# Normalised rows and projection weights as scaled float16 pairs, rows of all four token groups kept on chip

## The chip, the cores and the metric

The kernel runs on one core of a Trainium2 chip. The metric is the device time of one execution in microseconds. The core's engines have short names in the profile: PE is TensorE's matrix products (PEld its weight loads), DVE is VectorE, ACT is ScalarE, POOL is GpSimd, and SP issues the DMAs.

## The reference

Two layers over 2048 tokens of 1024 features. Each layer projects the normalised rows by one matrix, splits the result into a gated spatial part (u, v, g_A) and an attention part (q, k, v, g_B), and adds the normalised output projection to its input.

```python
for l in range(DEPTH):                       # DEPTH = 2, x is (1, 2048, 1024)
    h = rmsnorm(x, pre_g[l])                 # x / rms(x) * pre_g
    proj = jnp.einsum('bsd,de->bse', h, w_in[l])
    u_a, v_a, g_a, q, k, v, g_b = jnp.split(proj, idx, axis=-1)   # 512,512,512,512,128,128,512
    y_a = gmlp_group(u_a, v_a, ...) * jax.nn.silu(g_a)
    y_b = gqa_axial_attention(q, k, v, ...) * jax.nn.silu(g_b)    # 8 query heads, 2 kv heads
    out = jnp.einsum('bse,ed->bsd', jnp.concatenate([y_a, y_b], -1), w_out[l])
    x = x + rmsnorm(out, post_g[l])
```

Inside the attention q and k are RMS-normalised by head, multiplied by a gain and rotated (rope); `gmlp_group` applies a layer norm to v and mixes the 128 positions of a chunk by a 128x128 matrix per head. All of it is float32.

## The kernel before

A float32 operand of a product is kept as a pair, hi and lo, and a product is three passes, hi·hi, hi·lo and lo·hi (`PASSES`). In the projections both are of the type fp32r, four bytes each: ACT casts the high part and DVE subtracts it from the original for the low part.

The 2048 tokens are four groups of 512, each of four tiles of 128. `hT_jobs` prepares a group: a tile's rows (`x_t`, or `x_h` where the layer before has prepared them) are loaded, their squares summed by ACT, a reciprocal root found in tiny DVE instructions (`rs_x`, L133 to L137), and the rows multiplied by it and by `g_row`, the gain pre_g on every partition (L308). PE transposes them, ACT casts the result to `hT`, and DVE forms the low part (L319).

The projection weights come in blocks of 256 columns: K/V, two of Q, two of VA (v_a), two of GB (g_B), and four pairs of 128 columns of g_A and of u. `load_w` loads a block (`w_raw`), `split_w` splits it into `w_hi` (ACT, L276) and `w_lo` (DVE, L277), two instructions of 128x1024 each. `proj_tok` makes 24 products of 128x256 per tile and block, `proj_ch` 24 of 128x512 per group and 128 columns for the gates.

One layer goes through the tokens in two halves of two groups. A half's stages are: K/V and first Q block for each of its groups, second Q block, both VA blocks, both GB blocks, then the gate blocks; each half loads and splits every block anew. I call K/V and the two Q blocks the front. The next half's first group is prepared among the last gate blocks. Every stage ends in work on the other engines: `norm_rope` for K and Q has ACT square, DVE sum (L360), nine tiny DVE instructions, then the rope: a DVE product with PSUM (L367), a GpSimd product (L369), eight DVE products per tile pair on quarter rows (L372) and a DVE addition (L374), after which PE transposes the result. The tables of the rope are loaded and multiplied with a gain on GpSimd (L351).

A background list, `bg`, sets where much of that stands in the program: a job is added with a delay in ticks, and one tick passes after every eight products of `proj_tok` or four of `proj_ch`. Q's transposes have a delay of 16 (`Q_DELAY`), K's of 20 and more. Eight PSUM banks hold everything that PE produces, seven of them taken in turn. During the second half's GB and gate stages 128 products `pmax` and their maxima `mx` (L706) for the attention are mixed in. The attention and the output projection follow; at the end of layer 0 the last tiles are finished by GpSimd products with `g_post`, and rows of groups 0 and 1 are already normalised for layer 1 (`x_r`).

The functions that the change touches:

Of the kernel before, what the change touches and what calls it, by code (L numbers as in the profile page):

```python
# [19 lines left out]
P = 128  # L20
D = 1024
# [13 lines left out]
NORM_SCALE = -8192.0 / D ** 0.5  # L35


@with_exitstack
def encoder(ctx: ExitStack, tc, x, w_in, w_out, pre_g, post_g, ln_a_g, ln_a_b,
# [7 lines left out]
    HALF = min(2, NG)  # L47
# [49 lines left out]
    nc.vector.tensor_scalar_mul(two, two, 2.0)  # L97
    one_h = const.tile([P, 32], F16, name="one_h")
# [76 lines left out]
    class Project:  # L175
        def __init__(self, l):
            self.l = l
            self.stores = []
            self.g_row = None

        def norm_row(self):

            self.g_row = lay.tile([P, D], F32, name="g_row")
            if self.l == 0:
                for i in range(2):
                    sl = slice(i * GRP, (i + 1) * GRP)
                    one = f_t("g_one")[0:1]
                    nc.sync.dma_start(one, pre_g[self.l:self.l + 1, sl])
                    ps = ps_t("pt")
                    PE.matmul(ps, ones1, one, start=True, stop=True)  # L190
                    nc.vector.tensor_scalar(self.g_row[:, sl], ps, 1.0 / NORM_SCALE, None, ALU.mult)
                return
            nc.sync.dma_start(self.g_row, pre_g[self.l].partition_broadcast(P))
            nc.gpsimd.tensor_scalar(self.g_row, self.g_row, 1.0 / NORM_SCALE, None, ALU.mult)

        def begin(self):

            self.w_kv = self.split_w(self.load_w([C_K]), 2)

        def gains(self):  # L200
            l = self.l
            self.two = lay.tile([P, 32], F32, name="two_v")
            self.gain_q = lay.tile([P, 2, HD], F32, name="gain_q")
# [66 lines left out]
        def split_w(self, raw, n=4):  # L270

            hi = w_t([P, ND, WB], "w_hi")
            lo = w_t([P, ND, WB], "w_lo")
            for d in range(0, ND, n):
                sl = slice(d, d + n)
                nc.scalar.copy(hi[:, sl], raw[:, sl])  # L276
                nc.vector.tensor_tensor(lo[:, sl], raw[:, sl], hi.bitcast(F32)[:, sl], ALU.subtract)  # L277
            return hi, lo

        def hT_jobs(self, g, tail=False):  # L280

            hT = [big_t([P, 2, ND // 2, GRP], "hT") for _ in range(2)]
# [3 lines left out]
            def prep(j):  # L286
                def f():
# [10 lines left out]
                    if self.g_row is None:  # L298
                        self.norm_row()
# [7 lines left out]
                    for i in range(2):  # L307
                        nc.vector.scalar_tensor_tensor(xt[i], xt[i], z, self.g_row[:, i * GRP:(i + 1) * GRP],  # L308
                                                       ALU.mult, ALU.mult)
                return f  # L310

            def trans(j, q):
                def f():
                    ps = ps_t("pt").rearrange("p (d t) -> p d t", d=4)
                    for d in range(4):
                        PE.transpose(ps[:, d, :], xs[j][q][:, d * P:(d + 1) * P], ident)
                    sl = slice(j * P, (j + 1) * P)
                    act.copy(hT[q][:, 0, :, sl], ps)
                    dve.tensor_tensor(hT[q][:, 1, :, sl], ps, hT[q].bitcast(F32)[:, 0, :, sl], ALU.subtract)  # L319
                return f  # L320
            return hT, [prep(j) for j in range(TPG)], [trans(j, q) for j in range(TPG) for q in range(2)]

        def proj_tok(self, hT, j, w, ps=None, c0=0):
# [3 lines left out]
            for a, b in PASSES:  # L327
                for d in range(ND):
                    PE.matmul(ps[:, c0:c0 + WB], hT[d // 4][:, a, d % 4, j * P:(j + 1) * P], w[b][:, d, :],
                              start=(n == 0), stop=(n == 3 * ND - 1))  # L330
                    n += 1
                bg.tick()
            return ps

        def proj_ch(self, hT, w, c0):
            ps = ps_t("pp")
            n = 0
            for a, b in PASSES:
                for d in range(ND):
                    PE.matmul(ps, w[b][:, d, c0:c0 + P], hT[d // 4][:, a, d % 4, :],  # L340
# [13 lines left out]
        def norm_rope(self, banks, n, tb):  # L354
# [7 lines left out]
            nc.vector.tensor_scalar(msf, msf, 1.0 / HD, EPS, ALU.mult, ALU.add)  # L362
# [23 lines left out]
        def do_kv(self, g, banks):  # L386
            k_st, k_lo, v32, _ = self.kv
            b4 = [ps.rearrange("p (t h d) -> p t h d", t=2, d=HD) for ps in banks]
            for i, ps in enumerate(b4):
                t = g * TPG + 2 * i  # L390
                nc.scalar.copy(v32[:, t:t + 2], ps[:, :, 2:4])
            krs = self.norm_rope([ps[:, :, 0:2] for ps in b4], NKV, self.rope_rows(g, self.gain_k))
# [15 lines left out]
        def do_q(self, g, banks, b):  # L408
            qrs = self.norm_rope([ps.rearrange("p (t h d) -> p t h d", t=2, d=HD) for ps in banks], 4,
                                 self.rope_rows(g, self.gain_q))  # L410
# [55 lines left out]
        def do_gate(self, g, c, pg, pu):  # L466
# [3 lines left out]
            nc.scalar.activation(th, pg, AF.Tanh, scale=0.5)  # L470
            nc.vector.scalar_tensor_tensor(th, th, 1.0, pg, ALU.add, ALU.mult)
            nc.vector.tensor_tensor(th, pu, th, ALU.mult)
            nc.vector.scalar_tensor_tensor(th, th, 0.5, z, ALU.mult, ALU.mult)
# [7 lines left out]
        def do_gb(self, g, banks, b):  # L481
            for i, ps in enumerate(banks):
                th = f_t("fa")
                nc.scalar.activation(th, ps, AF.Tanh, scale=0.5)
# [4 lines left out]
        def scale_v(self):  # L489
# [18 lines left out]
            def scale():  # L508
# [5 lines left out]
                nc.vector.tensor_scalar(self.two, two, e, None, ALU.mult)  # L514

# [14 lines left out]
        def run(self, kv, first, last_jobs, first_wo):  # L530
# [3 lines left out]
            halves = [list(range(h, min(h + HALF, NG))) for h in range(0, NG, HALF)]  # L534
            w_kv = self.w_kv
            for n, gs in enumerate(halves):
                if len(gs) > 1:
                    hTs[gs[1]], preps, trans = self.hT_jobs(gs[1])
                    late = self.l == 0 and n == 0
                    for j, f in enumerate(preps):  # L540
                        if late:
                            bg.add(8 + j, f)
                        else:
                            f()
                    for m, f in enumerate(trans):
                        bg.add((13 if late else T_DELAY) + 3 * m // 2, f)
                if n == 0:
                    self.gains()
                raw = self.load_w([C_Q])
                if self.l == 0 and n == 0:  # L550
                    w = []
                    bg.add(8, lambda w=w, raw=raw: w.extend(self.split_w(raw)))
                else:
                    w = self.split_w(raw)
                for i, g in enumerate(gs):
                    if i == 0:
                        for f in self.stores:
                            f()
                        self.stores = []
                    if i == len(gs) - 1:  # L560
                        raw = self.load_w([C_Q + WB])
                    self.do_kv(g, self.banked(hTs[g], w_kv))
                    if i == len(gs) - 1:
                        w_next = self.split_w(raw)
                        raw = self.load_w([C_VA])
                    self.do_q(g, self.banked(hTs[g], w), 0)
                if n == 0:
                    self.spatial_weights()
                w = w_next
                for i, g in enumerate(gs):  # L570
                    self.do_q(g, self.banked(hTs[g], w), 1)
                    if i == 0:
                        w_next = self.split_w(raw)
                w = w_next
                raw = self.load_w([C_VA + WB])
                ws = [row_t("ws", dt=F32R) for _ in range(2)]
                for i in range(2):
                    nc.sync.dma_start(ws[i].bitcast(F32), ws_d[:, i])
                w = [w, self.split_w(raw)]
                raw = self.load_w([C_GB])  # L580
                for g in gs:
                    vs = []
                    for j in range(TPG):
                        ps = self.proj_tok(hTs[g], j, w[0])
                        self.proj_tok(hTs[g], j, w[1], ps, WB)
                        v = f_t("fv")
                        nc.scalar.copy(v, ps)
                        vs.append(v)
                    self.do_va(g, vs, ws)
                w = self.split_w(raw)  # L590
                blocks = [[C_GB + WB]] + [[C_GA + c * P, C_U + c * P] for c in range(4)]
                if n + 1 < len(halves):
                    blocks.append([C_K])
                if n + 1 == len(halves):
                    nc.gpsimd.memset(self.kv[1][HD:HD + 2], 1.0)
                    self.scale_v()
                    last_jobs()
                for b in range(2):
                    raw = self.load_w(blocks.pop(0))
                    for i, g in enumerate(gs):  # L600
                        self.do_gb(g, self.banked(hTs[g], w), b)
                        if i == 0:
                            w_next = self.split_w(raw)
                    w = w_next
                more = n + 1 < len(halves)
                order = [(c, i) for c in range(4) for i in range(len(gs))]
                if more:
                    order[-2 * len(gs):] = [(c, i) for i in range(len(gs)) for c in (2, 3)]
# [645 lines left out]
```

## Time and profile before

| | |
|---|---|
| median of 3 runs | 2741.04 us (2739.78 to 2742.96) |
| span of the profiled execution | 2737.6 us (the runs are 2 to 5 us above it) |
| PE busy | 2666.4 us, 97% |
| DVE busy | 1858.2 us, 68% |
| ACT busy | 1523.9 us, 56% |
| POOL busy | 1296.1 us, 47% |
| read from HBM, written | 176.57 MB, 85.07 MB |
| w_raw loads | 28 of 1024 KB, 32 of 512 KB |

Layer 0's projections lie between 17.6 and 616.2 us, layer 1's between 1383.5 and 1966.4 us, and what is left is attention and output projection. A busy time is the union of an engine's instructions; matrix products overlap, so that their mean duration (287 ns for 128x256) is longer than the distance at which one follows the other, and the distance is read from the starts in the timeline.

### The profile page before, as it was taken

The page shows a single profiled execution, that of the slowest core. Times are in us where ns is not written, and L with a number is a line of the kernel's source. Part 1 is how long each engine was busy: PE and PEld are TensorE (multiplying, and loading weights), DVE is VectorE, ACT ScalarE, POOL GpSimd, SP SyncE. Part 2 cuts the span into 40 slices and gives each one's busy share as a digit, 9 for nine tenths or more (in the row PEclk, how much of TensorE's full clock was granted, in tenths as well). Part 3 has the DMA queues.
Part 4 walks back from the last instruction along what each step waited for, and adds up shares of the span by engine and source line. Part 5 has one row for each costly group of instructions (what it writes and reads, how often), then busy time and mean ns, then how long its engine had stood idle before and what let it go on. Part 6 is the DMA issues. An engine that isn't in the chain of part 4 may idle for free.

```text
span 2737.6 us, 48445 instructions
## 1 busy us (share of the span) xinstructions
PE 2666.4 (97%) x18234; PEld 1773.2 (65%) x18234; DVE 1858.2 (68%) x3780; ACT 1523.9 (56%) x3023; POOL 1296.1 (47%) x1079
## 2 busy tenths in 40 slices
PE   7999999999999999999999999999999999999997
PEld 7998999764444444445599989997644444444444
DVE  7762888876666766666497538897766656666664
ACT  5221422118887777877642224221388878778774
POOL 1210121008786776777633011210377767767764
PEclk9999999999999999999999999999999999999998
DMA  4434422322232222222354434232312222221313
GB/s 137 149 98 122 161 80 84 107 75 84 81 91 66 76 84 84 90 81 84 125 169 138 122 115 144 74 121 71 109 51 81 79 71 70 83 75 48 114 46 132
DMA packets 275170, 264.78 MB, mean 97 GB/s; under 512 B 19188, under 2 KB 233332, under 8 KB 274936
## 3 DMA queue, kind: packets, MB, share of 16 engines
q1 hardware_dynamic: 274936, 261.70, 30.5%
q8 instruction: 143, 2.34, 0.4%
q14 instruction: 91, 0.75, 0.1%
HBM read 176.57 MB, written 85.07 MB: 96 GB/s over the span
## 4 chain that ended last, share of the span: by engine, by line
PE 81%; DVE 10%; ACT 5%; DMA 2%; issue 2%; POOL 1%; SPq 0%; DVEq 0%; POOLq 0%; ACTq 0%
PE pp L84 28%; PE sp L84 14%; PE pout L84 12%; PE po L84 12%; PE pmax L84 7%; PE sums L84 4%; PE pt L84 3%; ACT p_parts L84 2%; ACT p_f L84 2%; DVE fc L372 1%; DVE w_lo L277 1%; DVE mx L84 1%; DVE p_parts L84 1%; DVE o_t L84 1%; DVE mx L706 1%
## 5 line engine op out<-in xcount | busy, mean ns | idle before, releaser
L84 POOL TENSOR_TENSOR p_parts<-p_f,p_parts 128x512 f16<-128x512 f32 x872 | 1037.4, 1208 | 395.1 <-ACT p_f L84 295.5
L84 ACT ACTIVATE p_parts<-sp 128x512 f16<-128x512 f32 x1024 | 628.3, 614 | 295.7 <-PE sp L84 288.5
L84 DVE TENSOR_REDUCE mx<-pmax 128x1 f32<-128x512 f32 x768 | 511.2, 681 | 230.9 <-PE pmax L84 228.9
L84 PE MATMUL pout<-wo,y_t 128*128 128x512 f32 x1488 | 655.4, 504 | 1.0 <-ACT p_f L84 0.7
L84 PE MATMUL po<-p_parts,v_st 128*32 128x512 f16 (+1 forms) x3072 | 637.2, 382 | 0.2
L84 ACT ACTIVATE p_f<-sp 128x512 f32<-128x512 f32 x1024 | 629.9, 615 | 0.4 <-DVE p_parts L84 0.4
L84 PE MATMUL pp<-w_hi,hT 128*128 128x256 f32 x3584 | 496.7, 287 | 2.1 <-DVE k_t L405 1.1
L84 PEld LDWEIGHTS pp<-w_hi,hT 128*128 128x128 f32 x3584 | 457.3, 192 | 6.4 <-issue 1.3
L84 PE MATMUL pmax<-k_t,q_m 128*128 128x512 f16 x1024 | 388.9, 381 | 12.5 <-DVE mx L84 7.4
L84 PE MATMUL sp<-q_st,k_t 128*128 128x512 f16 x1024 | 389.2, 380 | 5.3 <-ACT p_f L84 2.9
L84 PEld LDWEIGHTS <-v_st 128*32 128x32 f16 (+1 forms) x3072 | 193.1, 96 | 308.4 <-issue 250.3
L84 PE MATMUL sp<-q,k_t 66*128 66x512 f16 x1024 | 390.1, 381 | 0.0
L84 PEld LDWEIGHTS pout<-wo,y_t 128*128 128x128 f32 x1488 | 280.7, 190 | 134.2 <-issue 14.9
L84 PEld LDWEIGHTS <-k_t 128*128 128x128 f16 (+1 forms) x2048 | 191.3, 98 | 184.1 <-issue 71.1
L477 POOL TENSOR_TENSOR fl<-fa,fh 128x512 fp32r<-128x512 f32 x32 | 42.7, 1335 | 539.6 <-ACT fh L476 496.0
L84 PE MATMUL pp<-hT,w_hi 128*128 128x512 f32 x1024 | 273.1, 413 | 0.0
L84 PE MATMUL pp<-w_lo,hT 128*128 128x256 f32 x1792 | 260.0, 288 | 0.0
L84 PE MATMUL sums<-p_parts,one_h 128*32 128x512 f16 x2048 | 241.8, 379 | 0.0
L84 PEld LDWEIGHTS pp<-w_lo,hT 128*128 128x128 f32 x1792 | 232.9, 192 | 1.0
L84 PEld LDWEIGHTS pp<-hT,w_hi 128*128 128x128 f32 x1024 | 192.8, 189 | 35.1
L706 DVE TENSOR_REDUCE mx<-pmax 128x1 f32<-128x512 f32 x256 | 172.5, 687 | 49.1 <-PE pmax L84 47.5
L84 PEld LDWEIGHTS <-q_m 128*128 128x128 f16 x1024 | 99.8, 98 | 142.6 <-issue 41.8
(165 smaller groups left out, 2778.1 us busy)
## 6 DMA issues: line engine op xcount, KB each, us to landing
w_raw<-in_w_in_dram SPq DMA_DIRECT2D x28, 1024.0 KB
y_t<-y_d SPq DMA_DIRECT2D x56, 512.0 KB
w_raw<-in_w_in_dram SPq DMA_DIRECT2D x32, 512.0 KB
x_t<-in_x_dram SPq DMA_DIRECT2D x16, 512.0 KB
z_d<-fb SPq DMA_DIRECT2D x32, 256.0 KB
gb_d<-fa SPq DMA_DIRECT2D x32, 256.0 KB
fb<-z_d SPq DMA_DIRECT2D x32, 256.0 KB
y_d<-fh SPq DMA_DIRECT2D x32, 256.0 KB
```

Source lines behind the costliest of these rows:

```text
L84: return tc.keep_in_program_order(call(*args, **kw))
L277: nc.vector.tensor_tensor(lo[:, sl], raw[:, sl], hi.bitcast(F32)[:, sl], ALU.subtract)
L372: nc.vector.tensor_tensor(t2[:, :, :, lo:lo + 16], qn[:, :, :, hi:hi + 16], tbi[:, :, 1:2, lo:lo + 16].broadcast_to([P, 2, n, 16]), ALU.mult)
L477: nc.gpsimd.tensor_tensor(lo, th, hi.bitcast(F32), ALU.subtract)
L706: dve.tensor_reduce(s.mx[:, j, c:c + 1], ps, AX.X, ALU.max)
```

## The change

1. Rows and weights of the projections are float16 pairs. `hT` is one tile [hi/lo, 8, 512] in place of two, so that four groups fit where two did. `w_hl` holds both parts of a block in half of the bytes.
2. `pre_g` no longer multiplies the rows (`g_row`) but the weights, as a column per partition (`g_col`, L277 after), on GpSimd but for one half of layer 0's first Q block.
3. Since float16 has a narrow range, each block is scaled by a power of two from its largest magnitude: two DVE reductions (L280), a DVE square, two tiny PE products with a constant (`pe`), and eight tiny DVE instructions (L289 to L303). ACT casts with that scale, DVE forms the low part with it (L295). What stands behind the projections takes the scale back (`w.u`, `w.hu`, `w.hu2`, `w.eps`, `two_g`).
4. Each block is loaded and split once per layer: a layer is now K/V and first Q block for all four groups, second Q block for all, VA for all, GB, gates. Group 2's rows are prepared in the front like the others. The part of `split_w` after the reductions is delayed by 14 ticks (`W_DELAY`).

```diff
-        def split_w(self, raw, n=4):
-            hi = w_t([P, ND, WB], "w_hi")
-            lo = w_t([P, ND, WB], "w_lo")
-            for d in range(0, ND, n):
-                sl = slice(d, d + n)
-                nc.scalar.copy(hi[:, sl], raw[:, sl])
-                nc.vector.tensor_tensor(lo[:, sl], raw[:, sl], hi.bitcast(F32)[:, sl], ALU.subtract)
-            return hi, lo
+        def split_w(self, raw, delay, vec=False):
+            w = Obj()
+            w.hl = w_t([P, 2, ND, WB], "w_hl", F16)
...
+            for i in range(2):
+                sl = slice(i * ND // 2, (i + 1) * ND // 2)
+                engine = nc.vector if vec and i == 0 else nc.gpsimd
+                g = self.g_col[:, sl].unsqueeze(2).broadcast_to([P, ND // 2, WB])
+                engine.tensor_tensor(raw[:, sl], raw[:, sl], g, ALU.mult)
+            for i in range(2):
+                sl = slice(i * ND // 2, (i + 1) * ND // 2)
+                nc.vector.tensor_reduce(top[:, i:i + 1], raw[:, sl].rearrange("p d e -> p (d e)"), AX.X, ALU.max,
+                                        apply_absolute_value=True)
+            nc.vector.tensor_tensor(sq, top, top, ALU.mult)
+
+            def rest():
+                ps = ps_t("pe")
+                for i in range(2):
+                    PE.matmul(ps[:, 0:1], spread_w, sq[:, i:i + 1], start=(i == 0), stop=(i == 1))
...
+                for i in range(2):
+                    sl = slice(i * ND // 2, (i + 1) * ND // 2)
+                    nc.scalar.activation(w.hl[:, 0, sl], raw[:, sl], AF.Copy, scale=w.e)
+                    nc.vector.scalar_tensor_tensor(w.hl[:, 1, sl].rearrange("p d e -> p (d e)"),
+                                                   raw[:, sl].rearrange("p d e -> p (d e)"), w.e,
+                                                   w.hl[:, 0, sl].rearrange("p d e -> p (d e)"),
+                                                   ALU.mult, ALU.subtract)
...
+            if delay is None:
+                rest()
+            else:
+                bg.add(delay, rest)
+            return w
 
         def hT_jobs(self, g, tail=False):
 
-            hT = [big_t([P, 2, ND // 2, GRP], "hT") for _ in range(2)]
+            hT = big_t([P, 2, ND, GRP], "hT", F16)
...
-                        nc.vector.scalar_tensor_tensor(xt[i], xt[i], z, self.g_row[:, i * GRP:(i + 1) * GRP],
-                                                       ALU.mult, ALU.mult)
+                        nc.vector.tensor_scalar(xt[i], xt[i], z, None, ALU.mult)
...
+            for i, g in enumerate(gs):
...
+                if i + 1 < NG:
+                    start(g + 1)
+                if i == 1:
+                    raw = self.load_w([C_Q + WB])
+                self.do_kv(g, self.banked(hTs[g], w_kv), w_kv)
+                if i == 2:
+                    w_next = self.split_w(raw, W_DELAY)
+                    raw = self.load_w([C_VA])
+                self.do_q(g, self.banked(hTs[g], w[0]), 0, w[0])
...
+            for i, g in enumerate(gs):
+                if i == 0:
+                    va = [self.split_w(raw, W_DELAY)]
+                    raw = self.load_w([C_VA + WB])
+                if i == 2:
+                    va.append(self.split_w(raw, W_DELAY))
+                    raw = self.load_w([C_GB])
+                self.do_q(g, self.banked(hTs[g], w), 1, w)
...
-                    return lambda: DVE.scalar_tensor_tensor(s.x[:, sl], s.o[:, sl], zh, nxt.g_row[:, sl],
-                                                            ALU.mult, ALU.mult)
+                    return lambda: DVE.tensor_scalar(s.x[:, sl], s.o[:, sl], zh, None, ALU.mult)
```

A scheduler sets the order on each engine, and it moves three places that matter here. On DVE at the start of the program, before: the low parts of K's weights stand among the steps of the first row's root.

```order
L191 TENSOR_SCALAR g_row<-pt 128x512
L277 TENSOR_TENSOR w_lo<-w_raw,w_hi 128x512
L133 TENSOR_SCALAR rs_m<-ss_x 128x1
L134 TENSOR_SCALAR rs_x<-rs_m 128x1
L136 TENSOR_SCALAR rs_t<-rs_x,rs_m 128x1
L277 TENSOR_TENSOR w_lo<-w_raw,w_hi 128x512
```

The same place after:

```order
L280 TENSOR_REDUCE w_col<-w_raw 128x1 x2
L282 TENSOR_TENSOR w_col<-w_col 128x2
L289 TENSOR_SCALAR w_col<-pe 128x1
L290 TENSOR_SCALAR w_col<-w_col 128x1
```

After those and the remaining tiny steps the two L295 follow, and the first row's root stands behind all of them; the reductions wait for GpSimd's product of the weights.

On GpSimd, in the front of layer 0, before: the rope table of K (`fa`), the filling of a constant, and the first rope products.

```order
L351 TENSOR_TENSOR fa<-fa,gain_k 128x512
L595 MEMSET k_t 2x4096
L369 TENSOR_TENSOR fc<-fc,fa 128x2x128 x2
L351 TENSOR_TENSOR fa<-fa,gain_q 128x512
L369 TENSOR_TENSOR fc<-fc,fa 128x512 x2
```

After (L382 is before's L351, L400 is L369, L643 is L595):

```order
L277 TENSOR_TENSOR w_raw<-w_raw,g_col 128x1024 x3
L382 TENSOR_TENSOR fa<-fa,gain_k 128x512
L277 TENSOR_TENSOR w_raw<-w_raw,g_col 128x1024 x2
L643 MEMSET k_t 2x4096
L277 TENSOR_TENSOR w_raw<-w_raw,g_col 128x1024 x2
L400 TENSOR_TENSOR fc<-fc,fa 128x2x128 x2
L382 TENSOR_TENSOR fa<-fa,gain_q 128x512
L400 TENSOR_TENSOR fc<-fc,fa 128x512 x2
```

K's weights and one half of Q0's come first, then Q1's and VA0's ahead of the first rope product.

On GpSimd, where layer 1 begins, before:

```order
L84 TENSOR_TENSOR o_t<-o_t,g_post 128x256 x16
L351 TENSOR_TENSOR fa<-fa,gain_k 128x512
L595 MEMSET k_t 2x4096
L369 TENSOR_TENSOR fc<-fc,fa 128x2x128 x2
L351 TENSOR_TENSOR fa<-fa,gain_q 128x512
```

And after:

```order
L84 TENSOR_TENSOR o_t<-o_t,g_post 128x256 x16
L277 TENSOR_TENSOR w_raw<-w_raw,g_col 128x1024 x2
L382 TENSOR_TENSOR fa<-fa,gain_k 128x512
L643 MEMSET k_t 2x4096
L277 TENSOR_TENSOR w_raw<-w_raw,g_col 128x1024 x3
L400 TENSOR_TENSOR fc<-fc,fa 128x2x128
```

Q0's products stand behind the 16 gains of layer 0's last tiles, and three of the four for Q1 and VA0 ahead of the first rope product.

More of the change, by code (lines that the diff above doesn't have):

```diff
@@ L178, in __init__, with norm_col @@
             self.stores = []
[L179 to L194, printed above, removed]
+            self.g_col = None
+        def norm_col(self):
+            self.g_col = lay.tile([P, ND], F32, name="g_col")
+            nc.sync.dma_start(self.g_col, pre_g[self.l].rearrange("(d p) -> p d", p=P))
         def begin(self):
-            self.w_kv = self.split_w(self.load_w([C_K]), 2)
+            raw = self.load_w([C_K])
+            if self.g_col is None:
+                self.norm_col()
+            self.w_kv = self.split_w(raw, None)
         def gains(self):
@@ new lines, in run, with start, one @@
+            gs = list(range(NG))
+            left = {}
+            def start(g):
+                hTs[g], preps, trans = self.hT_jobs(g)
+                left[g] = list(trans)
+                def one():
+                    if left[g]:
+                        left[g].pop(0)()
+                late = self.l == 0 and g == 1
+                for j, f in enumerate(preps):
+                    if late:
+                        bg.add(8 + j, f)
+                    else:
+                        f()
+                for m in range(len(trans)):
+                    bg.add((13 if late else T_DELAY) + 3 * m // 2, one)
@@ new lines, in run @@
+            nc.gpsimd.memset(self.kv[1][HD:HD + 2], 1.0)
+            self.scale_v()
+            last_jobs()
+            blocks = [[C_GA + c * P, C_U + c * P] for c in range(4)]
+            gbs = []
+            for b in range(2):
+                assert w.ready
+                gbs.append(w)
+                for i, g in enumerate(gs):
+                    self.do_gb(g, self.banked(hTs[g], w), b, w)
+                    if i == 1:
+                        w_next = self.split_w(raw, W_DELAY)
+                        raw = self.load_w(blocks.pop(0))
+                w = w_next
@@ new lines, in run @@
+            assert self.scaled
+            for b in range(2):
+                nc.vector.tensor_scalar(self.two_g[:, b], self.two, gbs[b].e, NORM_SCALE, ALU.mult, ALU.mult)
+            for c in range(4):
+                assert w.ready
+                for i, g in enumerate(gs):
+                    pg = self.proj_ch(hTs[g], w, 0)
+                    pu = self.proj_ch(hTs[g], w, P)
+                    self.do_gate(g, c, pg, pu, w)
+                    if i == 1 and c < 3:
+                        w_next = self.split_w(raw, W_DELAY)
+                        raw = self.load_w(blocks.pop(0)) if blocks else None
+                    if c == 3:
+                        hTs[g] = None
+                        if i == 1:
+                            first_wo()
+                w = w_next
@@ L635, in encoder @@
+            bg.flush()
     KK_DELAY = 20
@@ L749, in den @@
                 for c in range(4):
-                    PE.matmul(s.pd[32 * c:32 * c + 32, 0:TPG], layers[l].two, rows[:, :, c, 0], start=True, stop=True)
+                    PE.matmul(s.pd[32 * c:32 * c + 32, 0:TPG], layers[l].two_g[:, h // 4], rows[:, :, c, 0], start=True, stop=True)
             def rden():
```

194 lines of the change are left out of this document (77 added, 117 removed).

## Prediction

> **What bounds the kernel now.** I read the page first: the engine shares, the slices, the chain.
>
> ```profile
> PE 2666.4 (97%) x18234; PEld 1773.2 (65%) x18234; DVE 1858.2 (68%) x3780; ACT 1523.9 (56%) x3023; POOL 1296.1 (47%) x1079
> ...
> PE   7999999999999999999999999999999999999997
> ...
> DVE  7762888876666766666497538897766656666664
> ...
> PE 81%; DVE 10%; ACT 5%; DMA 2%; issue 2%; POOL 1%; SPq 0%; DVEq 0%; POOLq 0%; ACTq 0%
> ```
>
> TensorE is busy 97% and carries 81% of the chain, DMA 2%: halving the weight loads buys nothing by itself. But VectorE is high in slices 1 to 8 and 20 to 24, where the projections run. So the windows of the projection stages next: the start, then the four fronts (K/V and both Q blocks of a half), then the four value stages, then the GB and gate stages. Columns: stretch, its length, busy time of PE, PEld, DVE, ACT, POOL.
>
> ```profile
> 0.00:17.60 17.60, 5.47 (x12) 2.73 (x12) 8.88 (x33) 7.34 (x16) 0.69 (x6) 1.00 0.63 205
> ...
> 17.60:107.70 90.10, 83.47 (x674) 81.80 (x673) 80.11 (x225) 36.66 (x80) 23.52 (x16) 0.98 0.36 110
> 310.50:389.90 79.40, 76.34 (x641) 75.96 (x640) 70.92 (x183) 27.28 (x57) 22.06 (x16) 1.00 0.36 114
> 1383.50:1460.40 76.90, 76.90 (x650) 76.90 (x649) 70.00 (x183) 26.10 (x54) 25.80 (x22) 1.00 0.37 119
> 1663.10:1740.00 76.90, 76.15 (x641) 75.95 (x640) 69.28 (x176) 27.22 (x57) 19.26 (x15) 1.00 0.35 111
> sum 323.30, PE 312.86 PEld 310.62 DVE 290.31 ACT 117.26 POOL 90.63; mean PE 78.22 PEld 77.66 DVE 72.58 ACT 29.32 POOL 22.66
> ...
> sum 220.90, PE 220.11 PEld 214.45 DVE 157.24 ACT 59.98 POOL 47.17; mean PE 55.03 PEld 53.61 DVE 39.31 ACT 15.00 POOL 11.79
> ...
> 165.10:310.50 145.40, 144.12 (x860) 128.25 (x859) 70.91 (x158) 40.83 (x76) 15.32 (x11) 1.00 0.45 134
> 442.90:616.20 173.30, 172.52 (x967) 134.48 (x967) 142.65 (x258) 33.18 (x56) 15.37 (x11) 1.00 0.33 97
> ...
> sum 637.30, PE 633.16 PEld 525.37 DVE 427.04 ACT 147.92 POOL 62.21; mean PE 158.29 PEld 131.34 DVE 106.76 ACT 36.98 POOL 15.55
> ```
>
> Value, GB and gate stages are plain TensorE (853.3 of 858.2 us). The fronts have two near-bounds: TensorE 312.9 of 323.3 and VectorE 290.3. VectorE is even behind at their ends. The last rope addition (L374) starts 18.4 us after the last front's end at 1740.0, and the windows of these lags show what it then does:
>
> ```profile
> L374 DVE TENSOR_TENSOR fc<-fc x12: 408/674/680, 1683.2 to 1758.4; 128x512 f32<-128x512 f32 x8, 128x256 f32<-128x256 f32 x4
> ...
> 389.90:408.90 19.00, 18.74 (x158) 18.54 (x156) 17.82 (x41) 5.06 (x9) 5.98 (x4) 1.00 0.32 94
> ...
> sum 76.20, PE 75.62 PEld 69.91 DVE 65.64 ACT 27.77 POOL 26.08; mean PE 18.91 PEld 17.48 DVE 16.41 ACT 6.94 POOL 6.52
> ```
>
> Four times 65.64/4 = 16 us of front work is done under the value stage. I take 0.2% (5.5 us) as what a measurement here can tell from no change.
>
> **What TensorE gains.** Eight 256-column fp32r products start 0.96 us before the next eight, 120 ns each; sixteen of 512 columns 3.62 us, 226 ns each. Float16 is seen at 512 only: from 704.31 to 706.27 nine products, 218 ns each.
>
> ```profile
> 150.37 1.12 PE L84 MATMUL pp<-w_hi,hT 128*128 128x256 f32 x8
> 151.33 1.12 PE L84 MATMUL pp<-w_lo,hT 128*128 128x256 f32 x8
> ...
> 250.44 3.79 PE L84 MATMUL pp<-hT,w_hi 128*128 128x512 f32 x16
> 254.06 1.98 PE L84 MATMUL pp<-hT,w_lo 128*128 128x512 f32 x8
> ...
> 704.31 0.39 PE L84 MATMUL sp<-q_st,k_t 128*128 128x512 f16 x1
> ...
> 706.27 0.38 PE L84 MATMUL sp<-q,k_t 66*128 66x512 f16 x1
> ```
>
> So 8 ns less per product at 512. At 256 no row tells: 0 if nothing changes, 8 if the gain is a fixed part of each product, 11 if the product takes half of 218; I take 10. Outside the fronts a layer has 768 value and 768 GB products at 256 and 768 gate products at 512: 15.4 + 6.1 = 21.5 us, 43 for both layers. Group 2's 32 transposes leave the gate stage (the first GB/gate window holds them), at no more than the 120 ns of 256 columns some 3.5 us a layer: 7. The second GB/gate window is 27.9 us longer than the first for its 128 pmax products, which are float16 and worth 128 × 218 ns = 27.9, although the first has those 3.5 us of transposes more: so about 3.5 us a layer goes where the two types alternate, 0 to 7 in all, take 3. The attention's x_r loses its gain row: 16 times 1134 less 543 ns (rows below) on VectorE, mostly covered there by TensorE, 0 to 9, take 2. Sum **55 us** (22 to 70).
>
> **What the fronts lose.** Rows first, VectorE's and GpSimd's: groups of instructions (busy us, mean ns of one, idle before), three lines by tile (shortest/median/longest in ns, first and last start in us) and one of the timeline.
>
> ```profile
> L706 DVE TENSOR_REDUCE mx<-pmax 128x1 f32<-128x512 f32 x256 | 172.5, 687 | 49.1 <-PE pmax L84 47.5
> ...
> L277 DVE TENSOR_TENSOR w_lo<-w_raw,w_hi 128x1024 fp32r<-128x1024 f32 x84 | 104.1, 1253 | 17.2 <-ACT w_hi L276 16.0 <-PE pp L84 0.6
> L372 DVE TENSOR_TENSOR fc<-fc,fa 128x128 f32<-128x128 f32 x128 | 68.0, 590 | 16.3 <-POOL fa L351 15.7
> L308 DVE SCALAR_TENSOR_TENSOR x_t<-x_t,rs_x,g_row 128x512 f32<-128x512 f32 x48 | 37.6, 822 | 0.1
> L137 DVE TENSOR_SCALAR rs_x<-rs_t,rs_x 128x1 f32<-128x1 f32 x72 | 14.1, 210 | 0.7
> ...
> L84 DVE SCALAR_TENSOR_TENSOR x_r<-o_t,rs_o,g_row 128x512 f32<-128x512 f32 x16 | 18.1, 1134 | 0.0
> ...
> L277 DVE TENSOR_TENSOR w_lo<-w_raw,w_hi x92: 680/1218/1923, 10.9 to 1891.8; 128x1024 fp32r<-128x1024 f32 x84, 128x512 fp32r<-128x512 f32 x8
> ...
> L438 DVE TENSOR_SCALAR fv<-fv,mv_v,rs_y x32: 539/543/1529, 141.4 to 1800.6; 128x512 f32<-128x512 f32 x32
> L372 DVE TENSOR_TENSOR fc<-fc,fa x192: 209/279/1392, 54.9 to 1757.6; 128x128 f32<-128x128 f32 x128, 128x64 f32<-128x64 f32 x64
> ...
> L369 POOL TENSOR_TENSOR fc<-fc,fa 128x512 f32<-128x512 f32 x32 | 48.7, 1523 | 63.0 <-DVE fc L367 56.3 <-issue 6.1
> L477 POOL TENSOR_TENSOR fl<-fa,fh 128x512 fp32r<-128x512 f32 x32 | 42.7, 1335 | 539.6 <-ACT fh L476 496.0 <-issue 43.6
> ...
> 1375.33 11.94 POOL L84 TENSOR_TENSOR o_t<-o_t,g_post 128x256 f32<-128x256 f32 x15 [0.49 <-ACT pout L84]
> ```
>
> VectorE's work for all fronts before is 8.9 (start) + 290.3 + 65.6 (lags). The preparation of group 2, in the gate stage before, comes to stand in the front: the first GB/gate window has 70.9 of DVE, the second 142.7 with 128 maxima of 0.687 (88), so 54.7 without, and the first also holds one K split of 2 × 1.25: 13.7 us, 27.4 for both layers. Together 392.
>
> Out go 17 splits (five and four in layer 0, four and four in layer 1) of two w_lo of 1.253: −42.6. In come 9 of the new kind: two reductions of 1024 elements (0.7 to 1.4; take 1.2), two L295 of 1.25 as w_lo, nine tiny ones of 0.15 to 0.21 (1.5): 6.4 each, +57.6; and one weight product on VectorE, 1.3. The row scale x_t drops a vector operand: 822 to the 543 of fv, which also has one vector and per-partition scalars; 48 × 0.279 = −13.4.
>
> The gain products move to GpSimd: 17 in the fronts of 2 × 1335 = 2.7 us (2.4 to 3.3), 46 us. GpSimd has room, but VectorE pays: L372 takes 209 ns at best and 590 on average, 128 × 0.38 = 48.8 us lost beside 48.7 us of GpSimd's L369. There the two always meet; a weight product meets such two-operand work some 3 times in 10 (L372, L374 and the like are some 120 of 392 us): +14, bounds 0 and 46.
>
> The Trainium skill, page "SBUF — State Buffer", section "Who interferes with whom", says that a VectorE instruction with two SBUF inputs and a GpSimd instruction that reads SBUF take a port from one another for the whole instruction, and that one with a single SBUF input or a reduction does not; the L372 row agrees. By it the price reaches the upper bound if the scheduler puts each product ahead of two-operand work, a sum 34 us higher (rival 3); the order doesn't tell which meet.
>
> Sum of VectorE's work: 392 − 42.6 + 57.6 + 1.3 − 13.4 + 14 = **409 us**. TensorE's in the fronts is 312.9 − 2304 × 10 ns (768 + 384 a layer, all at 256) + 7 = 297. So VectorE becomes the bound there. When it is behind it is busy 17.82 of 19.0, 0.94: 409/0.94 = 435. It begins about 12.5: K's first w_lo started at 10.9, after a cast, and a product of 2.7 now stands in that place. The lag that the value stage can take is unchanged in kind (Q's transposes follow 16 ticks later and wait for L374), but there is one value stage per layer in place of two: 2 × 16 = 32 come off. At the start of layer 1 Q0's products stand behind the 16 gains on GpSimd, the last of which ends at 1387.3, and the K rope's L400 behind those and Q1's; TensorE has K/V of one group (96 × 110 ns) meanwhile; the Q0 block then waits for products, reductions and split: some 5 us (0 to 12). Fronts after: 12.5 + 435 − 32 + 5 = 420.5; before 17.6 + 323.3 = 340.9. Loss **80 us** (40 to 125).
>
> Other edits: the loads in layer 0 of Q1 and VA0 stand behind four row loads that wait for buffers, and K's first rope product waits on GpSimd behind both; L372, which follows it in the rope, first ran at 54.9 before, and two loads of 1 MB at the front's 110 GB/s take 19 us, so they land before that if issued by 35: nothing. Two tiny products per block on TensorE wait for the reductions 14 ticks later: nothing, since 14 ticks are 12 us. ACT's casts keep their number per split.
>
> **Sum.** −55 + 80 = +25 on the span of 2737.6: 2762.6. The median of the three runs, 2741.04, stands 3.4 above this span, so 2766.
>
> **Rivals.** (1) VectorE keeps up better, faster: fewer gaps (0.99) and no meeting on the port, 395/0.99 = 399, fronts 379, +38.5 − 55: 2724. For it: fronts before had it at 0.90 because TensorE gave the pace; against: 0.94 even when behind. It decides below 410 us of work over efficiency, where the fronts take 396 and both sums cancel, 25 us under mine. (2) TensorE stays the bound in the fronts: 297 + 22 for the start = 319, −22 − 55: 2664. VectorE's work would need to be a quarter smaller; the windows speak against. (3) Port fully paid, +32/0.94 = 34: 2800. (4) Float16 doesn't shorten 256-column products, so that part of the change doesn't do what it says: value and GB gain 31 us less: 2797. For it: no row at 256. (5) Both sums cancel: 2741.
>
> **Chances.** My forecast 0.46, own range 2747 to 2795; (1) 0.26; (2) 0.06; (3) 0.07; (4) 0.03; (5) 0.12. Faster (1, 2) 0.32, same (5) 0.12, slower 0.56. The range 2690 to 2805 leaves out (2), the tail of (1), and what lies beyond (3).
>
> **What would show it.** Right: in the K/V and Q stage of each layer DVE busy over 90% and PE clearly under (some 0.75), PE's waits there on DVE L405 and L350; that stage some 185 to 215 us a layer; value stages with no f32 pp, 256-column pitch near 110 ns; gate blocks of 48 products near 10.4 us instead of 10.9; L277 on POOL 2.4 to 3.3; mean of L403 above 590. Wrong: PE above 0.95 in the fronts (rivals 1, 2), a pitch of 120 (4), or a stall of TensorE on `pe` products, or of GpSimd on a weight load, over 10 us, which I have at nothing.

## The result and the profile after

The changed kernel takes 2789.06 us (median of 4 runs, 2788.33 to 2790.26) where the kernel before took 2740.41 beside it. The ratio is 1.0174, with a 95% interval of 1.0159 to 1.0188: slower by 49 us. The forecast was 2766, 25 us slower.

The page of the changed kernel: shares of the engines, and the slices of PE, DVE and the granted clock.

```profile
PE 2626.5 (94%) x18318; PEld 1543.7 (55%) x18318; DVE 1891.0 (68%) x3978; ACT 1500.0 (54%) x3007; POOL 1361.8 (49%) x1121
...
PE   5788999999999999999978889999999999999997
...
DVE  7978797435665766666498878983366656566664
...
PEclk9899999999999999999999999999999999999999
```

PE is busy 40 us less in a span that is 49 us longer. It is at 5 to 8 tenths in the first four slices and at 7 and 8 in the 21st to 24th, where the two layers begin. The clock's digit drops to 8 in the second slice only, but the windows below show 0.90 and 0.92 for both fronts (0.98 to 1.00 before). The windows of the changed kernel by stage: the start, the two fronts (K/V and Q blocks of four groups), then per layer the value stage, and GB with the gates. Columns as in the prediction: stretch, length, busy time of PE, PEld, DVE, ACT, POOL, granted clock.

```profile
0.00:26.20 26.20, 2.76 (x12) 2.50 (x12) 13.15 (x46) 7.34 (x14) 7.77 (x10) 1.00 0.62 196
26.20:235.10 208.90, 172.69 (x1393) 146.65 (x1393) 185.81 (x530) 77.99 (x180) 58.37 (x40) 0.90 0.31 95
1404.20:1611.20 207.00, 166.14 (x1370) 141.62 (x1369) 184.18 (x485) 69.93 (x156) 67.09 (x50) 0.92 0.32 99
...
235.10:347.60 112.50, 106.09 (x925) 93.74 (x923) 85.90 (x220) 24.31 (x51) 31.74 (x22) 0.97 0.22 62
347.60:637.30 289.70, 288.14 (x1755) 172.37 (x1754) 181.93 (x346) 53.28 (x83) 35.73 (x25) 1.00 0.29 84
...
sum 806.40, PE 788.98 PEld 532.56 DVE 535.19 ACT 155.07 POOL 135.08; mean PE 197.25 PEld 133.14 DVE 133.80 ACT 38.77 POOL 33.77
```

| stage, both layers | before | after | difference | forecast |
|---|---|---|---|---|
| start and fronts | 340.9 | 442.1 | +101.2 | +79.6 |
| value, GB, gates | 858.2 | 806.4 | −51.8 | −53 |
| span | 2737.6 | 2786.9 | +49.3 | +25 |

What is left between these sums (attention and output projection) is unchanged within 1 us. The loss in the fronts is a quarter larger than forecast. In the fronts DVE is busy 370.0 of 415.9 us and PE 338.8.

The gain behind the fronts came as forecast in its sum, but not in its parts. The two value stages together became 5.6 us longer (226.5 beside 220.9), where the terms of the forecast make them some 15 us shorter, and GB and gates became 57.4 us shorter (579.9 beside 637.3) in place of some 38. About 7 us of both comes from where the boundary lies: 29 of the 120 ns products a layer now stand before it. But in the two value stages TensorE also waits 13.7 us for VectorE's last rope additions (L405), and before it was busy 220.1 of 220.9 us there.

The float16 products can now be read in the timeline (start, length, count):

```profile
269.83 5.84 PE L84 MATMUL pp<-w_hl,hT 128*128 128x256 f16 x52
275.43 0.48 PE L84 MATMUL pt<-ws,fh 128*128 128x256 f32 x2
...
511.70 33.40 PE L84 MATMUL pp<-hT,w_hl 128*128 128x512 f16 x154
```

52 products of 256 columns take 5.60 us to the next instruction, 108 ns each (120 before); 154 of 512 columns 33.40 us less the last one's 0.38, 216 ns each (226 before).

### The profile page after: what moved, and what is told of

It reads as the page before. It is cut to its first block, busy times and chain, and to the rows that moved or that the text cites. A ratio compares the mean times of both kernels' runs of the same rounds, so it can differ in the third digit from the quotient of the medians.

```text
span 2786.9 us, 48753 instructions
## 1 busy us (share of the span) xinstructions
PE 2626.5 (94%) x18318; PEld 1543.7 (55%) x18318; DVE 1891.0 (68%) x3978; ACT 1500.0 (54%) x3007; POOL 1361.8 (49%) x1121
## 5 line engine op out<-in xcount | busy, mean ns | idle before, releaser
L84 PE MATMUL pp<-w_hl,hT 128*128 128x256 f16 x5376 | 675.5, 279 | 9.9 <-DVE hT L350 5.8
L84 PEld LDWEIGHTS <-hT 128*128 128x128 f16 x5376 | 527.7, 100 | 105.7 <-issue 14.0
L84 PE MATMUL pp<-hT,w_hl 128*128 128x512 f16 x1536 | 344.4, 379 | 0.0
L84 PEld LDWEIGHTS <-w_hl 128*128 128x128 f16 x1536 | 150.3, 98 | 179.0
L277 POOL TENSOR_TENSOR w_raw<-w_raw,g_col 128x1024 f32<-128x1024 f32 x43 | 82.6, 1942 | 246.9 <-DMA w_raw<-in_w_in_dram 232.9
L84 DVE TENSOR_TENSOR p_parts<-p_f,p_parts 128x512 f16<-128x512 f32 x152 | 130.3, 858 | 68.6 <-ACT p_f L84 59.3
```

Source lines behind the costliest of these rows:

```text
L84: return tc.keep_in_program_order(call(*args, **kw))
L277: engine.tensor_tensor(raw[:, sl], raw[:, sl], g, ALU.mult)
```

## The experiments

| run | what | median us | ratio to before, 95% interval |
|---|---|---|---|
| changed kernel | | 2789.1 | 1.0174 (1.0159 to 1.0188) |
| e1 | no gain products | 2755.7 | 1.0050 (1.0035 to 1.0065) |
| e2 | constant scale | 2805.5 | 1.0236 (1.0221 to 1.0252) |
| e3 | a fourth pass in the fronts | 2818.6 | 1.0279 (1.0262 to 1.0296) |
| e4 | two halves again | 2876.3 | 1.0491 (1.0475 to 1.0507) |
| e5 | float16 types alone in before | 2694.2 | 0.9829 (0.9815 to 0.9844) |
| e6 | types and four groups, plain split | 2754.0 | 1.0049 (1.0034 to 1.0064) |
| e7 | GB blocks in the fronts | 2762.6 | 1.0077 (1.0062 to 1.0092) |
| e8 | e6 and e7 | 2709.1 | 0.9889 (0.9872 to 0.9905) |
| e9 | rope rows loaded by ACT | 2782.3 | 1.0149 (1.0132 to 1.0166) |
| e10 | e2 with gains apart | 2798.3 | 1.0210 (1.0194 to 1.0225) |
| e11 | e5 with rope rows loaded by ACT | 2703.5 | 0.9865 (0.9850 to 0.9880) |
| e12 | gain products on ACT | 2764.6 | 1.0084 (1.0056 to 1.0111) |

My theory (A) was that VectorE's amount of work sets the length of the fronts, since the cover (a stage in which TensorE has work enough for VectorE to catch up) of a second value stage and of the gate stage is gone. The rivals were waits in queues (B) and the lower granted clock (C).

**e1: without the gain products.**

```diff
-            for i in range(2):
-                ...
-                engine.tensor_tensor(raw[:, sl], raw[:, sl], g, ALU.mult)
```

> The changed kernel without the products of the weights with pre_g (L277; the gain is left out of the computation). Theory A (VectorE's own work bounds the fronts): only what GpSimd takes from VectorE through the port goes, some 14 us of VectorE work in both fronts, so about 2775 us. Theory B (the fronts are long because instructions wait in queues: GpSimd behind loads and gains, TensorE behind the reductions, 17 us of waits of the small pe products in both fronts): these waits go, 2745 to 2765. Theory C (the lower granted clock, 0.90 and 0.92 in the fronts, makes TensorE slow by itself): unchanged, 2789.

Measured 2755.7, 33 us less. C is out as the main cause, since the clock in the fronts stayed at 0.92 and 0.91. The time lies inside B's range and is 19 us under A's figure, so A alone missed here. By windows the start is 7 us shorter (first projection at 19.0 in place of 26.2), the fronts 20 (396.2 in place of 415.9), the value stages 10. VectorE's instructions, changed kernel first, then e1 (groups, mean ns before the last bar):

```profile
L403 DVE TENSOR_TENSOR fc<-fc,fa 128x128 f32<-128x128 f32 x128 | 75.5, 648 | 18.7 <-POOL fa L382 18.4
...
L339 DVE TENSOR_SCALAR x_t<-x_t,rs_x 128x512 f32<-128x512 f32 x48 | 31.0, 675 | 0.1
...
L405 DVE TENSOR_TENSOR fc<-fc 128x512 f32<-128x512 f32 x32 | 24.8, 775 | 0.0
...
L403 DVE TENSOR_TENSOR fc<-fc,fa 128x64 f32<-128x64 f32 x64 | 21.4, 393 | 0.3
```

```profile
L398 DVE TENSOR_TENSOR fc<-fc,fa 128x128 f32<-128x128 f32 x128 | 67.0, 582 | 21.1 <-POOL fa L377 21.1
...
L334 DVE TENSOR_SCALAR x_t<-x_t,rs_x 128x512 f32<-128x512 f32 x48 | 23.5, 520 | 0.1
...
L400 DVE TENSOR_TENSOR fc<-fc 128x512 f32<-128x512 f32 x32 | 21.6, 676 | 0.0
...
L398 DVE TENSOR_TENSOR fc<-fc,fa 128x64 f32<-128x64 f32 x64 | 18.8, 351 | 0.1
```

These four groups are 152.7 us with the products and 130.9 without: 22 us that VectorE lost while GpSimd ran beside it, where I had 14. The row scale x_t, which has one operand in SBUF, pays too (675 for 520). The Trainium skill, page "SBUF — State Buffer", section "Who interferes with whom", lists `tensor_scalar` among the instructions that can take GpSimd's port in a faster mode; the rows agree. The prediction's summary of that section left this exception out and counted every instruction with a single SBUF operand as free.

**e2: a constant scale, and e10: the same with gains apart.**

```diff
-                nc.vector.tensor_reduce(top[:, i:i + 1], raw[:, sl]..., AX.X, ALU.max, apply_absolute_value=True)
-                ... (the pe products and the tiny instructions)
+            col = fixed_col            # scale 1024, set once
 # e10 as well:
-            self.gain_q = lay.tile([P, 2, HD], F32, name="gain_q")
+            self.gain_q = lay.tile([P, 2, HD], F32, name=f"gain_q{l}")      # gain_k too
```

> The changed kernel with a constant scale of 1024 in place of the scale found from each block: no reductions, no pe products, no tiny instructions per block. Theory A: 9 blocks in the fronts times (2 x 1.206 + 9 x 0.15) = 34 us of VectorE work less, by 0.89 some 38 us: 2751, with the other stages unchanged. Theory B: 17 us of waits for pe go, 2772. Theory C: 2789.

> e2 again (constant scale, no reductions and tiny instructions), with tiles of their own for each layer's q and k gains, so that VectorE does not stand 12.7 us behind the load of layer 1's gain, which waited for layer 0's last use, in the middle of layer 0. Theory A: 34 us of VectorE work less in the fronts than the changed kernel, by 0.89 some 38 us: 2745 to 2765. If the scale's instructions cost nothing because others wait in their place: 2785 to 2806.

Measured 2805.5 and 2798.3: both slower than the changed kernel, though the edit takes out some 34 us of VectorE's instructions in the fronts. Theory A missed here. e2 had one stall that has nothing to do with the scale. VectorE's waits in its first value group:

```profile
DVE gain_q L221 <- DMA gain_q<-in_q_norm_g_dram: 12.7, 1, 12.7
```

The scheduler had put layer 1's gains there. e10 takes this away and gains 7 us. Its start and fronts are 435.7 us beside the changed kernel's 442.1, so only 6 us shorter, and VectorE is busy 368.8 us in them beside 383.1: 14 us less and not 34. The 9 us by which e10 is slower come from elsewhere: its GB and gate stages take 12 us more, and there TensorE waits 5.4 us a layer for inputs of the spatial products, for which it did not wait in the changed kernel. These stages of e10, then of the changed kernel:

```profile
sum 592.10, PE 579.02 PEld 343.23 DVE 332.37 ACT 94.42 POOL 56.35; mean PE 289.51 PEld 171.61 DVE 166.19 ACT 47.21 POOL 28.17
```

```profile
sum 579.90, PE 576.24 PEld 344.75 DVE 364.31 ACT 106.51 POOL 71.46; mean PE 288.12 PEld 172.37 DVE 182.16 ACT 53.25 POOL 35.73
```

Where VectorE's share of the 34 us went is seen in its groups over the whole of e10:

```profile
L285 DVE SCALAR_TENSOR_TENSOR w_hl<-w_raw,fixed_col,w_hl 128x1024 f16<-128x1024 f32 x44 | 61.3, 1395 | 21.2 <-ACT w_hl L284 20.7
...
L324 DVE TENSOR_SCALAR x_t<-x_t,rs_x 128x512 f32<-128x512 f32 x48 | 33.4, 720 | 0.2 <-DVE rs_x L142 0.2
...
L388 DVE TENSOR_TENSOR fc<-fc,fa 128x64 f32<-128x64 f32 x64 | 33.3, 579 | 0.4
```

Against the changed kernel (1279, 675 and 393 ns) these three cost 5, 2 and 12 us more, and the L285 group waits 21.2 us (L295 in the changed kernel 5.4). That GpSimd's products now meet other work on VectorE is my reading of the longer instructions and was not tested. How much the scale costs by itself stays open, since e10 has an order of its own.

**e3: a fourth pass in the fronts.**

```diff
+    FOUR = PASSES + ((1, 1),)
-                self.do_kv(g, self.banked(hTs[g], w_kv), w_kv)
+                self.do_kv(g, self.banked(hTs[g], w_kv, FOUR), w_kv)      # and both Q blocks
```

> The changed kernel with a fourth pass (lo times lo) in the K/V and Q blocks alone: 384 products of 128x256 a layer more, 84 us of TensorE at 109 ns in both layers, nothing else. Theory A: TensorE waits some 77 us in the two fronts, so most of it hides: fronts longer by 0 to 30 us, 2789 to 2819, DVE busy as before. Theory C: the granted clock rises to 0.97 or more, and the time hardly changes or falls. If TensorE bounds the fronts: 2870.

Measured 2818.6, 30 us more for 84 us of products. The fronts of e3, as a sum of their windows, and the changed kernel's:

```profile
sum 449.50, PE 407.75 PEld 358.38 DVE 377.59 ACT 151.88 POOL 138.40; mean PE 203.88 PEld 179.19 DVE 188.79 ACT 75.94 POOL 69.20
```

```profile
sum 415.90, PE 338.83 PEld 288.27 DVE 369.99 ACT 147.92 POOL 125.45; mean PE 169.42 PEld 144.13 DVE 184.99 ACT 73.96 POOL 62.73
```

50 of 84 us disappear in time in which TensorE waited anyhow. TensorE is not the bound alone, as A had it, but not free either: a third of the added products lengthens the fronts. The clock rose to 0.96 and 0.95 without making the fronts shorter, so C falls as the main cause; how much of the fronts' length a lower clock adds was not separated.

**e4: two halves again, with the new split.**

```diff
+            halves = [[0, 1], [2, 3]]
+            for n, gs in enumerate(halves):     # stages as before; every block loaded and split in each half
```

> The changed kernel with the loop over two halves as before (part 4 undone): float16 pairs, gains in the weights and scales stay, every block is loaded and split twice per layer. Theory A: VectorE has 8 more splits of 6.4 us in the fronts (+51), group 2's preparation goes back to the gate stage (-27) and two value stages per layer take the lag (-32): the fronts come out at 435 to 450 us beside 442 now, the whole at 2775 to 2800. If the grouping itself cost the time (lost cover, not VectorE's new work): 2700 to 2740.

Measured 2876.3, 87 us slower than with four groups and far above either figure. With 22 splits more, this is the slowest kernel of all. But the halves are not all that differs: most splits here are delayed by 8 ticks in place of 14, and there are fewer products to hide them. TensorE's waits in e4:

```profile
PE pe L84 <- DVE w_col L282: 58.3, 4, 17.0
PE pp L84 <- ACT w_hl L294: 55.1, 24, 8.8
PE pp L84 <- DVE w_hl L295: 21.4, 8, 8.1
```

In the changed kernel the first is 26.3 us and the other two don't occur. That is some 108 us more in which TensorE stands before blocks whose split isn't done, so e4 doesn't price the grouping by itself.

**e5: the float16 types alone, and e6: types and four groups with the plain split.**

```diff
 # e5, in the kernel before
-            hi = w_t([P, ND, WB], "w_hi")                  # lo and hT too
+            hi = w_t([P, ND, WB], "w_hi", F16)
 # e6, in the changed kernel: norm_row, g_row and L308 of before, and
+                    nc.scalar.copy(w.hl[:, 0, sl], raw[:, sl])
+                    nc.vector.tensor_tensor(w.hl[:, 1, sl], raw[:, sl], w.hl[:, 0, sl], ALU.subtract)
```

> The kernel before with float16 pairs in place of fp32r for rows and projection weights, and nothing else: two halves, gain in the rows, plain split without a scale. Theory A (TensorE gains 55 us outside the fronts, and VectorE holds the fronts): 2741 - 55 - 0 to 15 = 2670 to 2690. If 256-column products didn't gain: about 2715. If the type itself cost something: 2741 or more.

> The changed kernel's loop over four groups and its float16 pairs, with the plain split of before (cast and subtraction, no scale, no reductions, no pe products) and the gain in the rows as before. Theory A: VectorE's work in the fronts falls from 409 to 372 us, GpSimd has no weight products: fronts some 50 us shorter than in the changed kernel, 2725 to 2745; slower than the halves with the same split (e5) by some 50 us, because one value stage in place of two covers VectorE. If the new split alone was to blame and grouping is free: equal to e5 or below, 2660 to 2680.

Measured 2694.2 and 2754.0. The types gain 47 us, a little less than theory A's 51 to 71; the grouping with a plain split then costs 60, more than the types gain, and 2754.0 lies 9 us above A's range. The fronts of e5 (four windows) and of e6 (two):

```profile
sum 320.70, PE 297.13 PEld 262.59 DVE 286.44 ACT 116.08 POOL 90.13; mean PE 74.28 PEld 65.65 DVE 71.61 ACT 29.02 POOL 22.53
```

```profile
sum 385.00, PE 327.61 PEld 282.19 DVE 333.46 ACT 151.07 POOL 93.69; mean PE 163.81 PEld 141.09 DVE 166.73 ACT 75.54 POOL 46.84
```

In e5 they are as long as before (323.3), though TensorE's work there fell from 312.9 to 297.1: VectorE holds them. In e6 they are 64 us longer, and VectorE is busy 47 us more in them, with 8 splits fewer: group 2's preparation and the work that two value stages took. That is the price of the grouping with nothing of the new split in it. e5 is faster than both kernels. In this order the change is −47 for the types, +60 for the groups and +35 for gains and scale in the split (2789.1 less 2754.0), 48 in all. The parts depend on that order: with halves (e4 less e5) the new split costs 182.

**e7: GB blocks between the K/V and Q blocks, and e8: the same in e6.**

```diff
                 self.do_q(g, self.banked(hTs[g], w[0]), 0, w[0])
+                if i == 0:
+                    gbs[0] = self.split_w(raw_g, W_DELAY)
+                else:
+                    gb(0, g - 1)               # and gb(1, g - 1) behind the second Q block
```

> The changed kernel with another order of the same work: GB blocks, which need little of VectorE (some 1.4 us a group beside 10.6 of TensorE), stand group by group between the K/V and Q blocks in place of behind the value blocks. TensorE then has 297 + 170 us of work in the stage beside VectorE's 409 + 11. Theory A: VectorE's excess is covered, 40 to 60 us less than the changed kernel: 2730 to 2750. Theory B (waits in queues, not amount of work): 2775 to 2790.

> e6 and e7 together: float16 pairs, four groups, plain split with the gain in the rows, GB blocks between the K/V and Q blocks. Theory A: 2660 to 2700, the fastest of these with e5. Theory B: as e6.

Measured 2762.6 and 2709.1, 26 and 45 us less than the same work in the old order (the changed kernel and e6). That is less than A expected of either and more than B. Little but the order differs (e7 also has nine buffers for the scales in place of five): blocks that ask little of VectorE, put between those that ask much, shorten the whole, which fits A in part. They gain more with the plain split; why was not separated.

**e9 and e11: rope rows loaded by ACT.**

```diff
-            nc.sync.dma_start(cs.rearrange("p t a d -> p t (a d)"),
+            nc.scalar.dma_start(cs.rearrange("p t a d -> p t (a d)"),
```

> The changed kernel with the loads of the rope rows (L380) issued by ACT in place of SP, so that they no longer stand behind the stores of q that wait for VectorE and the weight loads. In the changed kernel VectorE waits some 10 us in the fronts and more behind them for GpSimd's product with these rows, whose loads land late, and TensorE waits 6 to 7 us at each first value group. Theory B (waits in queues): these waits go, 2765 to 2778. Theory A (amount of VectorE work alone): 2785 to 2790, the waits are taken by others.

> e5 (float16 types in the kernel before, nothing else) with the rope rows loaded by ACT. VectorE waits 3 to 5 us per front for them in the kernel before. Theory B: 2675 to 2688, the fastest so far. Theory A: 2690 to 2695.

Measured 2782.3 and 2703.5. In e9 VectorE's waits for GpSimd's rope product leave the list of its waits, yet the time falls by only 7 us, between the two ranges, and the intervals of the two ratios overlap. In e11 the time rises by 9; there was little to win, since in e5's first front VectorE had waited for that product only 2.0 us. Neither theory had a rise, and its cause stays open.

**e12: the gain products on ACT.**

```diff
-                engine.tensor_tensor(raw[:, sl], raw[:, sl], g, ALU.mult)
+            for d in range(ND):
+                nc.scalar.activation(raw[:, d], raw[:, d], AF.Copy, scale=self.g_col[:, d:d + 1])
```

> The changed kernel with the products of the weights with pre_g on ACT (eight activations of 128x256 per block with the gain as their scale) in place of GpSimd; nothing is left out. In e1, without these products, VectorE's two-operand instructions were shorter by 22 us in all (L403 582 in place of 648 ns, L339 520 in place of 675, L405 676 in place of 775) and the time 33 us less. If it is GpSimd's use of VectorE's port and GpSimd's own queue that cost this: 2755 to 2768, with L403 and L339 at e1's means. If it is that every block has to wait for one more step before its split, on whatever engine: 2780 to 2795, since eight activations take longer than two products (some 3 us beside 3.8) and ACT has its own work.

Measured 2764.6, with runs from 2756.6 to 2772.3. VectorE's groups are at e1's durations:

```profile
L400 DVE TENSOR_TENSOR fc<-fc,fa 128x128 f32<-128x128 f32 x128 | 67.1, 582 | 23.8 <-POOL fa L379 23.7
...
L336 DVE TENSOR_SCALAR x_t<-x_t,rs_x 128x512 f32<-128x512 f32 x48 | 23.8, 525 | 0.1
```

So some 25 of e1's 33 us (17 to 32 by the single runs) come from where the product runs and not from its being there. That includes both the shorter instructions and the place in GpSimd's queue, which this run doesn't separate.

## Why the prediction was right, and where its terms were off

**What TensorE gains.** 8 ns was read from rows at 512 columns and 10 taken at 256; it is 10 and 12. That the stages behind the fronts gave 51.8 us where the sum had 53 is partly luck. At 12 and 10 ns the products alone are worth 52 us there, transposes and the change between types come on top, and TensorE's new waits of 13.7 us in the value stages, which the sum had at nothing, take it down again. The types alone, e5, gave 46.5 us of span, 43 of them outside the start and the fronts, so little of TensorE's gain in the fronts counts, as was argued.

**VectorE becomes the bound of the fronts.** e3 (three fifths of added TensorE work hidden), e6 (64 us longer fronts with the same types) and e7 and e8 (shorter with blocks that ask little of VectorE in between) support it. It is not a pure bound: e10 takes out VectorE's work and hardly shortens the fronts, and the signs that I named came in part only. DVE was busy 0.89 of the fronts (over 0.90 forecast), PE 0.83 and 0.80 (some 0.75), and PE's longest waits were for `w_col` (L282) and `k_t` (L436), not for L405 and L350. TensorE was busy 338.8 us where the sum had 297; the lower clock, or products that stand alone and count with their full duration (279 ns on average), could make this up, and no run separates them. As a sum of work the 409 us were close: DVE was busy 13.15 us in the start, 370.0 in the fronts and 32.6 in the two stretches up to its last L405 (247.3 and 1638.7), 416. The parts of that were less good. GpSimd's meetings with VectorE cost 22 us where I took 14, and the scale of x_t, put at 543 ns, came to 675 for that reason.

**The mis-sized terms** are the efficiency and the starts. I divided the work by 0.94, the share of VectorE in one of the four lags. That was the better end of the rows: the sum of all four beside it, 65.64 of 76.20, is 0.86. In the two fronts it was 370.0 of 415.9, 0.89, and 409/0.89 − 409/0.94 is 24 us more, about the 22 that the forecast of the fronts fell short. VectorE waited there for work of others, and TensorE for it. Waits of PE in the front of layer 1 (us, times, longest):

```profile
PE pe L84 <- DVE w_col L282: 14.0, 1, 14.0
PE pt L84 <- DVE k_t L436: 9.0, 4, 4.7
PE pt L84 <- DVE fc L398: 5.7, 5, 2.7
```

The first of these is the stall at the start of layer 1 that I put at 5 us (0 to 12) and on GpSimd's gains. The timelines of POOL, DVE and PE there have

```profile
1403.42 5.52 POOL L84 TENSOR_TENSOR o_t<-o_t,g_post 128x256 f32<-128x256 f32 x8
1408.89 3.75 POOL L277 TENSOR_TENSOR w_raw<-w_raw,g_col 128x1024 f32<-128x1024 f32 x2
...
1408.33 6.85 DVE L84 SCALAR_TENSOR_TENSOR o_t<-o_t,rs_o,x_w 128x512 f32<-128x512 f32 x4
...
1418.45 3.73 DVE L84 SCALAR_TENSOR_TENSOR o_t<-o_t,rs_o,x_w 128x512 f32<-128x512 f32 x4
1422.11 1.21 DVE L280 TENSOR_REDUCE w_col<-w_raw 128x1 f32<-128x1024 f32 x1
...
1404.22 5.40 PE L84 MATMUL pp<-w_hl,hT 128*128 128x256 f16 x48
1423.65 0.56 PE L84 MATMUL pe<-w_col,spread_w 128*128 128x1 f32 x2 [14.03 <-DVE w_col L282]
```

GpSimd's products end at 1412.6, but VectorE makes the second reduction at 1422.11 only, because it finishes layer 0's last tiles first. In e1 the gain products are left out, and TensorE still waits 10.4 us at this place:

```profile
PE pe L84 <- DVE w_col L277: 10.4, 1, 10.4
```

So most of the stall is VectorE's order. What GpSimd adds is about the 3.7 us by which the four `o_t` that run beside its products are longer (6.85 us, 3.14 in e1). Two readings of the program were wrong here. Only 48 of the 96 K/V products stand ahead of the `pe` products, and this block's delay is 6 ticks and not 14, so that the `pe` products could not be put at nothing. A stall of TensorE on them over 10 us was one of my signs of being wrong, and it came. So did the other, GpSimd behind a weight load (21.6 us in the front of layer 0), but the first rope product after it waited for VectorE and not for GpSimd.

The first projection started at 26.2 (17.6 before); the sum let VectorE begin at 12.5 and had no term for TensorE's start.

**The other prices.** One L277 on GpSimd took 1.94 us (I took 2.7); a reduction 1.21 (1.2); an L295 1.28 (1.25). The last two were right; L277 came out below its range of 2.4 to 3.3. 17 products at 1.94 are 33 us of GpSimd, so by e1's 22 us VectorE lost about two thirds of a microsecond per microsecond of GpSimd, not the three tenths that I took.

**The rivals.** That VectorE keeps up, or TensorE stays the bound (1, 2), or both sums cancel (5): fronts that are 101 us longer exclude them. The fully paid port (3) forecast 2800, nearer to 2789 than my 2766, but not for its reason: VectorE paid 22 us, between my 14 and its 46 and nearer mine, and what lengthened the fronts beyond my sum was the efficiency. e1 and e12 put port and queue together at 25 to 33 us. That float16 doesn't shorten 256 columns (4): 108 ns.

## What to carry to other kernels

When a busy engine is made faster, look at each stage for the engine that is second, and ask what covers it: here two changes for TensorE's sake took away a cover and added work where VectorE was already 90% busy, while the type alone (e5) gave 47 us. Work for a spare GpSimd isn't free to VectorE: its price is paid in VectorE's instructions, and ACT was the better place here (e12). Put blocks that need little of the second engine between those that need much of it (e7, e8).

## What the runs showed that I had not expected

- Less work can take longer where a scheduler orders it: with some 34 us of VectorE's instructions taken out of the fronts, e10 is 9 us slower than the changed kernel. Its start and fronts are only 6 us shorter (a 128x64 rope product takes 579 in place of 393 ns), and its GB and gate stages are 12 us longer.
- The granted clock was lower where TensorE waited more: 0.90 and 0.92 in these fronts, 0.98 to 1.00 before, and 0.96 and 0.95 with a third more products (e3). What it cost was not measured.
- A per-partition scale (x_t, one operand in SBUF) is slowed by GpSimd as well, 675 in place of 520 ns on average, with one of 3810 ns.
